# Sums of W_out made behind the memory in the first stage, in place of the second stage

## The chip, the cores and the metric

One core of one Trainium2 chip runs the whole kernel. The metric is the device time of one launch in microseconds (us). Three runs of the kernel before took 629.17, 630.27 and 633.15 us; the median is 630.27. The engines are named PE (TensorE), DVE (VectorE), ACT (ScalarE), POOL (GpSimd) and SP (SyncE, which here only issues transfers).

## The reference

One layer over 2048 tokens of width 1024, all in float32:

```
hn    = rms_norm(x) * norm_g
u | mq | gate = hn @ w_in                 # 768 | 256 | 1024 columns
tok   = pooled windows (2, 4, 8, 16) of u, minus u, times w_group, times scale
mem_o = softmax(mq @ mem_k.T / 8) @ mem_v # 4 heads, 256 memory rows
y     = x + (concat(tok, mem_o) * silu(gate)) @ w_out
out   = rms_norm(y) * final_g
```

## The kernel before, in words

Float32 products are made of three products of reduced parts: each operand is split into a high part (a cast, `_split`, mostly on ACT at L38) and a low part (a difference on DVE, L46), and PE does high x high, high x low and low x high (L51, L52, L53). So each tile of weights has to pass through ACT and DVE before PE can use it.

The tokens are four blocks of 512. Stage 1 projects blocks 0 and 1 tile by tile (`TILES`, `tile_in`): queries q, gates g and pooled columns z, each tile with 48 products of 128x512 for the two blocks. Stage 2 projects blocks 2 and 3 (`project_in`, `group`), two tiles at a time with seven products in place of eight, and then come the two output projections, the second again with seven products (`project_out_by_products`). Sums of W_out that four of those seven need are made by `stage_weights` and kept in DRAM as `t_d`; the matching sums of the input columns of blocks 2 and 3 are made by `stage_forms` during stage 1, after `row_stats` has made the norms of those blocks from squares on ACT (L221).

After each half tile a counter (`Steps`) is advanced, and side work hangs on its values through `hooks`: the norms of blocks 0 and 1, the fold of w_group into the projection (`w_z`), the memory's keys and values (`memory`, at 17), the norms of the second pair (`stats`), its forms (`stage`), and the attention steps. In this program the order of the source is not the order on an engine: a scheduler places all instructions by a simulated timeline. On the chip each engine then works through its own list strictly in order, and so do the DMA queues of SP, ACT and POOL. [...]

`load` makes the scheduler issue its transfers in the order of the calls. `slot(n)` names one of fourteen large buffers x0 to x13, `zz` one of four smaller ones. `gate` tiles end in a Silu on ACT (`take_gate`, L496 to L499), z tiles in window sums on POOL (L523) and DVE (L532, L538). Attention is scores (L581, L582), maximum (L584), exponentials (L588), division (L591, L593), transposes (L604), split (L606) and the product with the values (L616).

In the order of the tiles, g3 follows the memory, then come z5, g2, z4.

Of the kernel before, what the change touches and what calls it, by code (L numbers as in the profile page):

```python
# [8 lines left out]
F32 = mybir.dt.float32  # L9
# [6 lines left out]
P = 128  # L16
# [3 lines left out]
KH = KT // 2  # L20
BT = 512
# [20 lines left out]
def _split(nc, hi, lo, src, hi_eng, lo_eng="dve"):  # L42

    _cast(nc, hi_eng, hi, src)
    e = nc.gpsimd if lo_eng == "pool" else nc.vector
    return e.tensor_tensor(out=lo, in0=src, in1=hi.bitcast(F32), op=ALU.subtract)  # L46


def _mm3(nc, ps, ahi, alo, bhi, blo, start, stop, **kw):

    nc.tensor.matmul(ps, lhsT=ahi, rhs=bhi, start=start, stop=False, **kw)  # L51
    nc.tensor.matmul(ps, lhsT=ahi, rhs=blo, start=False, stop=False, **kw)  # L52
    nc.tensor.matmul(ps, lhsT=alo, rhs=bhi, start=False, stop=stop, **kw)  # L53
# [3 lines left out]
def trunk(ctx, tc, x, xT, mem, memT, norm_g, mem_norm_g, w_mem, w_out, w_in, w_uT, w_g, p_scale, final_g,  # L57
# [6 lines left out]
    sp = nc.sync  # L64
# [19 lines left out]
    def slot(n, shape=(P, KH, BT), dt=F32R):  # L84
        return sl.tile(list(shape), dt, name=f"x{n}")

    def zz(shape, dt=F32):

        n = 1
        for v in shape[1:]:  # L90
            n *= v
        t = zw.tile([P, HALO + D], dt, name="zz")[:, :n]
        if len(shape) == 3:
            t = t.rearrange("p (a b) -> p a b", a=shape[1])
        return t
# [22 lines left out]
    def load(**kw):  # L118

        if not last:  # L120
            last.append(sp.dma_start(**kw))
        else:
            with tc.issue_after(last[-1].ins):
                last.append(sp.dma_start(**kw))
        return last[-1]
# [71 lines left out]
    def rstd_of(ssq, n):  # L197
        v = small.tile([P, QT], F32, name="var")
        nc.vector.tensor_scalar(v[:, :n], ssq, 1.0 / D, EPS, ALU.mult, ALU.add)
        r = small.tile([P, QT], F32, name="rstd")  # L200
        nc.gpsimd.tensor_tensor(out=r[:, :n], in0=v[:, :n], in1=half[:, :n], op=ALU.pow)
        return r

    def bcast_cols(r, n, dst, rb=None):

        ps = (ps_t if n == QT else ps_mm).tile([P, BT], F32, name="pt" if n == QT else "mm")
        rb = (sgp.tile([P, BT], F32, name="sg") if rb is None else rb)[:, :n * P].rearrange("p (t f) -> p t f", t=n)
        nc.vector.tensor_copy(rb, r[:, :n].unsqueeze(2).broadcast_to([P, n, P]))
        for t in range(n):
            nc.tensor.matmul(ps[:, t * P:(t + 1) * P], lhsT=rb[:, t, :], rhs=ident, start=True, stop=True)  # L210
        nc.vector.tensor_copy(dst, ps[:, :n * P])
# [29 lines left out]
    def combine(b11, b12, b21, b22, t1, t2, t4):  # L241

        g = nc.vector
        sub(g, t1, b12, b11)
        sub(g, t2, b22, t1)
        sub(g, b12, b22, b12)
        sub(g, t4, b21, t2)
# [34 lines left out]
    def x_slots(ps):  # L282
        return {p: tuple(slot(n) for n in PLACE[p]) for p in ps}
# [71 lines left out]
    def memory_norm(loaded):  # L355
        ssm = small.tile([P, 2], F32, name="ssm", bufs=1)
        for t in range(2):
            nc.scalar.activation(out=loaded[1][t], in_=loaded[1][t], func=AF.Square, accum_out=ssm[:, t:t + 1])
        loaded.append(rstd_of(ssm, 2))

    def memory(loaded):
        mh, ml = ([zz((P, 4, NMEM), F32R) for _ in range(2)] for _ in range(2))
        wrs, _, rm = loaded
        for c in range(2):
            mt = mts[c]
            for kk in range(4):
                k = 4 * c + kk
                g = gm[:, k:k + 1]
                nc.scalar.mul(mh[c][:, kk, :], mt[:, kk, :], g)
                nc.vector.scalar_tensor_tensor(out=ml[c][:, kk, :], in0=mt[:, kk, :], scalar=g,  # L370
                                               in1=mh[c][:, kk, :].bitcast(F32), op0=ALU.mult, op1=ALU.subtract)
        pk = [pl.tile([P, NMEM], F32, name=n) for pl, n in ((ps_s, "sc"), (ps_t, "pt")) for _ in range(2)]
        for c in range(4):
            wr = wrs[c]
            for kk in range(2):
                k = 2 * c + kk
                hi, lo = chunk(wr[:, kk, :], "pool")
                xh, xl = mh[k // 4][:, k % 4, :], ml[k // 4][:, k % 4, :]
                for p in range(2):
                    w = slice(p * P, (p + 1) * P)  # L380
                    _mm3(nc, pk[p], hi[:, w], lo[:, w], xh, xl, k == 0, k == KT - 1)
                for t in range(2):
                    w = slice(t * P, (t + 1) * P)
                    _mm3(nc, pk[2 + t], xh[:, w], xl[:, w], hi[:, NMEM:], lo[:, NMEM:], k == 0, k == KT - 1)
        rmb = sgp.tile([P, BT], F32, name="sg")[:, :NMEM]
        bcast_cols(rm, 2, rmb)
        nc.vector.tensor_scalar_mul(rmb, rmb, 0.125)
        for p in range(2):
            kf = att.tile([P, NMEM], F32, name="pr")
            nc.vector.tensor_tensor(out=kf, in0=pk[p], in1=rmb, op=ALU.mult)  # L390
            for h in range(2):
                r, o = slice(64 * h, 64 * h + 64), slice(64 - 64 * h, 128 - 64 * h)
                _split(nc, khi[r, p, h, :], klo[r, p, h, :], kf[r], "act")
                nc.gpsimd.dma_start(out=khi[o, p, h, :].bitcast(F32), in_=khi[r, p, h, :].bitcast(F32))
                nc.gpsimd.dma_start(out=klo[o, p, h, :].bitcast(F32), in_=klo[r, p, h, :].bitcast(F32))
        for t in range(2):
            vf = att.tile([P, NMEM], F32, name="pr")
            nc.vector.tensor_scalar_mul(vf, pk[2 + t], rm[:, t:t + 1])
            src = vf.rearrange("p (a h d) -> p a h d", a=2, h=2)
            for h in range(2):  # L400
                hi, lo = slice(64 * h, 64 * h + 64), slice(64 - 64 * h, 128 - 64 * h)
                _split(nc, vhl[:, t, :, h, hi], vhl[:, t, :, h, lo], src[:, :, h, :], "act")

    def chunk(src, hi_eng, shape=(P, BT), lo_eng="dve"):

        hi = ch.tile(list(shape), F32R, name="wh")
        lo = ch.tile(list(shape), F32R, name="wl")
        _split(nc, hi, lo, src, hi_eng, lo_eng)
        return hi, lo
# [277 lines left out]
    def y_later(p):  # L687
        y_slots(p)
        for k in range(0, KH, 2):
            rt = raw_tile((P, 2, BT))  # L690
            sp.dma_start(out=rt, in_=ys_d[k:k + 2, :, LATER.index(p), :].rearrange("k p t -> p k t"))
            for kk in range(2):
                _split(nc, Y[p][0][:, k + kk, :], Y[p][1][:, k + kk, :], rt[:, kk, :], "act")

    def stage_weights(k):

        r = []
        for kk in (k, k + KH):
            r.append(zz((P, 2, BT)))
            for dh in range(2):  # L700
                sp.dma_start(out=r[-1][:, dh, :], in_=w_out[kk // 2, dh, :, kk % 2, :])
        t = zz((P, 2, BT))
        t4 = sgp.tile([P, BT], F32, name="sg")
        b11, b12, b21, b22 = r[0][:, 0, :], r[0][:, 1, :], r[1][:, 0, :], r[1][:, 1, :]
        combine(b11, b12, b21, b22, t[:, 0, :], t[:, 1, :], t4)
        for i, v in enumerate((t[:, 0, :], t[:, 1, :], b12, t4)):
            nc.gpsimd.dma_start(out=t_d[i, k // 2, :, k % 2, :], in_=v)
# [154 lines left out]
    loaded = []  # L862
# [27 lines left out]
    def stats(a):  # L890
        if not a:
            load(out=ci, in_=cinv)
            state["rows"] = dram.tile([2, QT, P], F32, name="rows")
        row_stats(1, a, state["rows"])

    def stage(k):
        if not X1:
            X1.update(x_slots((1, 6, 2)))
        stage_forms(1, k, state["rows"], X1)
# [6 lines left out]
    def norm(a):  # L906
        first_norm(a)
        for f in unscaled[a]:
            f()

    hooks = {7: [lambda: norm(0)], 10: [lambda: norm(1)], 12: [fold, lambda: ahead.append(load_tile(w_in[6], load)), lambda: loaded.extend(load_memory())],
             14: [lambda: load_memory_rest(loaded)],
             15: [lambda: memory_norm(loaded)], 17: [lambda: memory(loaded)], 19: [lambda: stats(0)], 21: [lambda: stats(1)]}
    for k in range(KH):
        hooks[25 + 9 * k] = [lambda k=k: stage(k)]
    steps = Steps(0, 21, 2.4, hooks)
    xs = {0: first_block(0)}
    for kind, j, blocks in TILES:
# [30 lines left out]
            branch(s, e, *bhl[s], lambda: (zz if by == "zz" else raw_tile)((P, 2, BT)))  # L949

    hooks = {NP - 4: [lambda: bring(0, 0, (0, 1, 2, 3), "zz")], NP - 2: [lambda: bring(0, 1, (4, 5, 6, 7), "zz")]}
    for k, n in enumerate((12, 26, 30, 34)):
        hooks[n] = [lambda k=k: stage_weights(k)]
    project_in(1, X1, Steps(1, 10, 2, hooks))

    AT_CHUNK = {(0, 2): 0, (0, 3): 1, (1, 0): 2, (1, 1): 3}
# [51 lines left out]
```

## Time and profile before

| | |
|---|---|
| median of three runs | 630.27 us |
| profiled execution | 632.58 us |
| its span | 630.3 us |
| mean granted TensorE clock | 0.973 |
| PE busy | 592.0 us, 94% of the span |
| DVE busy | 452.8 us, 72% |
| ACT busy | 336.0 us, 53% |
| POOL busy | 160.3 us, 25% |

The span is the time from the first to the last instruction; some 2 us of the device time lie around it. An engine's busy time counts its instructions alone. A wait in square brackets behind a row of a timeline is the time that the engine stood idle before that instruction, and the instruction or transfer that released it. [...]

### The profile page before, as it was taken

The numbers are of one execution on the slowest core, as the hardware profiler recorded it, in microseconds if no ns is written. First come the engines' busy times: TensorE is split into PE (matmuls) and PEld (weight loads), VectorE is DVE, ScalarE is ACT, GpSimd is POOL, SyncE is SP. The second block draws the span as 40 slices with busy tenths as digits, with TensorE's granted clock in tenths as the row PEclk, the third lists the DMA queues.
The fourth block names the chain that finished last, engine by engine and source line by source line (L and its number), as shares of the span: only waits on it lengthen the run. The fifth ranks groups of instructions, "written<-read, shape, count | busy, mean of one in ns | idle before, by whom it ended". The sixth has DMA issues, their size and how long they took to land. (4 is left out here: it accounts for less than half of the span.)

```text
span 630.3 us, 8543 instructions
## 1 busy us (share of the span) xinstructions
PE 592.0 (94%) x2798; PEld 490.9 (78%) x2798; DVE 452.8 (72%) x754; ACT 336.0 (53%) x696; POOL 160.3 (25%) x181
## 2 busy tenths in 40 slices
PE   7989779989989999999998899989899999999993
PEld 4879669868768888888886788868688888887882
DVE  6470246599786768897779888798785842969776
ACT  6825545446464664664963789634553511516442
POOL 0021114263442304101048212354100000304065
PEclk9999969999989999999999899989899999999998
DMA  8949995366465943668441986345999474799606
GB/s 314 391 166 338 393 356 170 117 198 227 161 236 160 319 146 112 234 219 294 165 112 48 294 296 216 125 145 198 353 359 351 135 244 144 236 358 344 221 19 248
DMA packets 63311, 144.34 MB, mean 229 GB/s; under 512 B 7714, under 2 KB 16674, under 8 KB 63268
## 3 DMA queue, kind: packets, MB, share of 16 engines
q1 hardware_dynamic: 53620, 122.30, 57.4%
q10 hardware_dynamic: 6832, 12.60, 5.4%
q0 software_dynamic: 2816, 8.92, 3.7%
q8 instruction: 22, 0.36, 0.2%
q14 instruction: 21, 0.17, 0.1%
HBM read 98.17 MB, written 45.09 MB: 227 GB/s over the span
## 5 line engine op out<-in xcount | busy, mean ns | idle before, releaser
L51 PE MATMUL mm<-x,wh 128*128 128x512 f32 x480 | 192.1, 402 | 11.1 <-ACT wh L38 8.2
L52 PE MATMUL mm<-x,wh 128*128 128x512 f32 x480 | 190.8, 398 | 0.6 <-DVE x L230 0.6
L53 PE MATMUL mm<-x,wl 128*128 128x512 f32 x480 | 189.7, 399 | 0.3 <-DVE wl L46 0.3
L46 DVE TENSOR_TENSOR wl<-raw,wh 128x512 fp32r<-128x512 f32 x116 | 86.6, 753 | 68.2 <-ACT wh L38 67.9
L38 ACT CAST wh<-raw 128x512 fp32r<-128x512 f32 x116 | 70.5, 617 | 89.7 <-PE pt L53 28.3
L51 PEld LDWEIGHTS mm<-x,wh 128*128 128x128 f32 x480 | 92.5, 193 | 31.2 <-ACT wh L38 8.6
L523 POOL TENSOR_TENSOR zz<-zz 128x527 f32<-128x527 f32 (+6 forms) x64 | 82.1, 1293 | 102.4 <-DVE zz L550 42.5
L52 PEld LDWEIGHTS mm<-x,wh 128*128 128x128 f32 x480 | 92.3, 192 | 19.8 <-DVE x L230 1.7
L53 PEld LDWEIGHTS mm<-x,wl 128*128 128x128 f32 x480 | 92.2, 192 | 19.4 <-DVE wl L46 1.1
L53 PE MATMUL mm<-wh,x 128*128 128x512 f32 x128 | 49.8, 389 | 0.0
L52 PE MATMUL mm<-wl,x 128*128 128x512 f32 x128 | 49.8, 389 | 0.0
L51 PE MATMUL mm<-wh,x 128*128 128x512 f32 x128 | 46.8, 390 | 2.0 <-ACT wh L38 2.0
L588 ACT ACTIVATE pr<-sc,nm 128x256 f32<-128x256 f32 x64 | 29.9, 472 | 29.9 <-DVE nm L584 26.0
L38 ACT CAST x<-raw 128x512 fp32r<-128x512 f32 x40 | 23.8, 617 | 37.6 <-DMA raw<-ys_d 12.4
L753 POOL TENSOR_TENSOR rstdo<-sso,half 128x1 f32<-128x1 f32 x16 | 12.7, 796 | 111.6 <-DVE sso L745 111.6
L593 ACT ACTIVATE pr<-pr,rc 128x256 f32<-128x256 f32 x64 | 29.1, 504 | 21.7 <-DVE rc L591 21.5
L46 DVE TENSOR_TENSOR x<-raw,x 128x512 fp32r<-128x512 f32 x40 | 32.8, 834 | 8.0 <-ACT x L38 8.0
L51 PEld LDWEIGHTS mm<-wh,x 128*128 128x128 f32 x128 | 24.0, 188 | 7.3 <-ACT wh L38 2.4
L52 PEld LDWEIGHTS mm<-wl,x 128*128 128x128 f32 x128 | 24.0, 188 | 5.0
L53 PEld LDWEIGHTS mm<-wh,x 128*128 128x128 f32 x128 | 24.0, 188 | 5.0
L604 PE MATMUL pt<-ident,pr 128*128 128x128 f32 x128 | 21.7, 288 | 6.2 <-ACT pr L593 6.1
L604 PEld LDWEIGHTS pt<-ident,pr 128*128 128x128 f32 x128 | 15.9, 146 | 11.3 <-ACT pr L593 8.7
(188 smaller groups left out, 1068.1 us busy)
## 6 DMA issues: line engine op xcount, KB each, us to landing
raw<-in_w_in SPq DMA_DIRECT2D x19, 512.0 KB, 6.1
x<-in_x SPq DMA_DIRECT2D x16, 512.0 KB, 7.6
g_d<-sg ACTq DMA_DIRECT2D x32, 256.0 KB, 3.4
raw<-in_w_out SPq DMA_DIRECT2D x14, 512.0 KB, 4.4
raw<-w_z SPq DMA_DIRECT2D x12, 512.0 KB, 4.6
sg<-g_d SPq DMA_DIRECT2D x24, 256.0 KB, 3.2
br_d<-zz SPq DMA_DIRECT2D x12, 512.0 KB, 4.3
x<-in_xT SPq DMA_DIRECT2D x8, 512.0 KB, 7.6
```

Source lines behind the costliest of these rows:

```text
L38: return nc.scalar.copy(hi, src)
L46: return e.tensor_tensor(out=lo, in0=src, in1=hi.bitcast(F32), op=ALU.subtract)
L51: nc.tensor.matmul(ps, lhsT=ahi, rhs=bhi, start=start, stop=False, **kw)
L52: nc.tensor.matmul(ps, lhsT=ahi, rhs=blo, start=False, stop=False, **kw)
L53: nc.tensor.matmul(ps, lhsT=alo, rhs=bhi, start=False, stop=stop, **kw)
L523: nc.gpsimd.tensor_tensor(out=cur[rows, c0:c1], in0=prev[rows, c0:c1], in1=prev[rows, c0 - step:c1 - step], op=ALU.add)
L588: nc.scalar.activation(out=pr[:, h, :], in_=ps[:, h, :], func=AF.Exp, bias=nm[:, h:h + 1], accum_out=su[:, h:h + 1])
L593: nc.scalar.mul(pr[:, h, :], pr[:, h, :], rc[:, h:h + 1])
L604: nc.tensor.transpose(ps[:, 2 * h + kt, :], pr[:, h, kt * P:(kt + 1) * P], ident)
L753: nc.gpsimd.tensor_tensor(out=ro, in0=self.sso[:, 1, t:t + 1], in1=half[:, :1], op=ALU.pow)
```

## The change

`stage_weights(k)` for k = 0 to 3 is called at step 18 of stage 1, four times in a row, right after the memory; before, it was called at steps 12, 26, 30 and 34 of stage 2. It takes its input from slots x8, x9, x11 and x13 and puts the sums into x10 and x12, which are empty at that time, and not into `zz` buffers; its loads go through `load`. The norms of the second pair move from steps 19 and 21 to 22 and 24, and its forms from steps 25, 34, 43 and 52 to 29, 37, 45 and 53. Nothing is added or left out: the same loads, differences and stores are made.

```diff
+    sums = []
+
     def stage_weights(k):
 
-        r = []
-        for kk in (k, k + KH):
-            r.append(zz((P, 2, BT)))
+        b = slot((8, 9, 11, 13)[k], (P, 2, 2, BT), F32)
+        r = [b[:, i] for i in range(2)]
+        for kk, v in zip((k, k + KH), r):
             for dh in range(2):
-                sp.dma_start(out=r[-1][:, dh, :], in_=w_out[kk // 2, dh, :, kk % 2, :])
-        t = zz((P, 2, BT))
+                load(out=v[:, dh, :], in_=w_out[kk // 2, dh, :, kk % 2, :])
+        if k % 2 == 0:
+            sums.append(slot((10, 12)[k // 2], (P, 2, 2, BT), F32))
+        t = sums[-1][:, k % 2]
         t4 = sgp.tile([P, BT], F32, name="sg")
...
-             15: [lambda: memory_norm(loaded)], 17: [lambda: memory(loaded)], 19: [lambda: stats(0)], 21: [lambda: stats(1)]}
+             15: [lambda: memory_norm(loaded)], 17: [lambda: memory(loaded)], 18: [lambda: [stage_weights(k) for k in range(KH)]],
+             22: [lambda: stats(0)], 24: [lambda: stats(1)]}
     for k in range(KH):
-        hooks[25 + 9 * k] = [lambda k=k: stage(k)]
+        hooks[29 + 8 * k] = [lambda k=k: stage(k)]
...
-    for k, n in enumerate((12, 26, 30, 34)):
-        hooks[n] = [lambda k=k: stage_weights(k)]
```

The scheduler's lists move around tile z5 and the tile after it, g2. On ACT before, from the cast of the second half of g3 (`wh_958`) to g3's second gate; `wh_1025` and `wh_1098` are z5's weights, `wh_1182` g2's, `x12` and `x13` rows of block 3, `sg_1013` a gate:

```order
L38 CAST wh_958<-raw_734 128x512
L221 ACTIVATE x12_1061,ss_1068<-x12_1061 128x1024
L38 CAST wh_1025<-raw_1021 128x512
L221 ACTIVATE x13_1064,ss_1068<-x13_1064 128x1024
L38 CAST khi_165<-pr_914 64x256 x2
L38 CAST khi_165<-pr_924 64x256 x2
L38 CAST wh_1098<-raw_1021 128x512
L221 ACTIVATE x13_1064,ss_1068<-x13_1064 128x1024
L38 CAST wh_1182<-raw_1178 128x512
L38 CAST vhl_167<-pr_934 128x2x64 x2
L38 CAST vhl_167<-pr_940 128x2x64 x2
L498 ACTIVATE sg_1013<-sg_1013 128x512
```

On ACT now, from the same gate (`sg_1044`) to the first cast of g2's weights (`wh_1240`):

```order
L498 ACTIVATE sg_1044<-sg_1044 128x512
L221 ACTIVATE x11_1109,ss_1113<-x11_1109 128x1024
L221 ACTIVATE x11_1109,ss_1113<-x11_1109 128x1024
L588 ACT_TABLE_LOAD
L588 ACTIVATE pr_1154,su_1155<-sc_1147,nm_1152 128x256 x2
L498 ACT_TABLE_LOAD
L593 ACTIVATE pr_1154<-pr_1154,rc_1158 128x256 x2
L221 ACTIVATE x12_1183,ss_1190<-x12_1183 128x1024
L221 ACTIVATE x13_1186,ss_1190<-x13_1186 128x1024
L38 CAST pth_1162<-pt_1164 128x4x128
L588 ACT_TABLE_LOAD
L38 CAST wh_1240<-raw_1236 128x512
```

The rows left out between these are more of the same kinds: in all there stand between the gate and that cast six squares, three pairs of exponentials, three pairs of scalings, three table loads, a second Silu and one cast of probabilities. Before, the cast of g2's weights stood ahead of the gate, and all squares of the second pair ahead of both gates.

On DVE now, from the last differences of `stage_weights` (L102) to the product that the gate's Silu waits for (`sg_1044`, L496); `wl_1057` and `wl_1132` are the low parts of z5's weights, `zz_1208` takes z5's result for the first block (`mm_1054`):

```order
L102 TENSOR_TENSOR x13_1002<-x13_1002 128x512
L398 TENSOR_SCALAR pr_934<-pt_776,rstd_712 128x256
L398 TENSOR_SCALAR pr_940<-pt_777,rstd_712 128x256
L46 TENSOR_TENSOR wl_1057<-raw_1052,wh_1056 128x512
L46 TENSOR_TENSOR wl_1132<-raw_1052,wh_1131 128x512
L46 TENSOR_TENSOR vhl_167<-pr_934,vhl_167 128x2x64 x2
L46 TENSOR_TENSOR vhl_167<-pr_940,vhl_167 128x2x64 x2
L102 TENSOR_TENSOR sg_1007<-x13_1002,x12_992 128x512
L550 TENSOR_TENSOR zz_1208<-mm_1054,u_322 128x512
L496 TENSOR_TENSOR sg_1044<-mm_736,u_322 128x512
```

Before, the same product (`sg_1013<-mm_736`) stood ahead of the copy of z5's first block (`zz_1150<-mm_1023`), with ten rows between them; now it stands behind it.

On SP before, the transfers from z5's weights (`raw_1021`) to the first column load of the second pair; `raw_1178` are g2's weights:

```order
L124 DMA raw_1021<-w_z_164 128x1024
L124 DMA x12_1061<-in_x 128x1024 x2
L124 DMA x13_1064<-in_x 128x1024 x2
L124 DMA raw_1178<-in_w_in 128x1024
L265 DMA raw_1245<-in_xT 128x2x512
```

On SP now, from the first loads of W_out to g2's weights (`raw_1236`):

```order
L124 DMA x9_973<-in_w_out 128x512 x4
L124 DMA x11_987<-in_w_out 128x512 x4
L124 DMA x13_1002<-in_w_out 128x512 x4
L124 DMA raw_1052<-w_z_164 128x1024
L124 DMA ci_162<-in_cinv 128x96
L124 DMA x10_1106<-in_x 128x1024 x2
L124 DMA x11_1109<-in_x 128x1024 x2
L124 DMA x12_1183<-in_x 128x1024 x2
L124 DMA x13_1186<-in_x 128x1024 x2
L124 DMA raw_1236<-in_w_in 128x1024
```

The rows of blocks 2 and 3 now go into slots in which W_out and its sums have been, so their loads wait until these have been stored.

## Rows read from the trace of the kernel before

**Rows 1.** Page, part 1: engine, busy us, share of the span, instructions.

```profile
PE 592.0 (94%) x2798; PEld 490.9 (78%) x2798; DVE 452.8 (72%) x754; ACT 336.0 (53%) x696; POOL 160.3 (25%) x181
```

**Rows 2.** What PE waited for over the whole span: us in total, times, longest.

```profile
PE pt L604 <- ACT pr L593: 6.1, 3, 2.9
PE sc L616 <- DVE ptl L46: 5.0, 2, 2.7
```

**Rows 3.** Windows of 10 us: busy us by engine, then granted clock, DMA share, GB/s.

```profile
80.00:90.00 10.00, 6.49 (x25) 5.55 (x26) 4.08 (x8) 5.42 (x10) 0.00 (x0) 0.58 0.99 358
140.00:150.00 10.00, 10.00 (x43) 8.34 (x43) 9.71 (x18) 5.16 (x12) 0.56 (x1) 0.85 0.60 188
```

**Rows 4.** Timeline of PE at the memory: start, us, operation, [idle before <- releaser].

```profile
83.51 0.80 PE L51 MATMUL mm<-x,wh 128*128 128x512 f32 x1 [8.20 <-ACT wh L38]
...
87.94 0.58 PE L52 MATMUL mm<-x,wh 128*128 128x512 f32 x1
88.36 0.39 PE L53 MATMUL mm<-x,wl 128*128 128x512 f32 x1
88.59 0.39 PE L51 MATMUL mm<-x,wh 128*128 128x512 f32 x1
```

**Rows 5.** Timeline of ACT at the memory.

```profile
82.42 0.33 ACTq L499 DMA_DIRECT2D g_d<-sg  x1
82.84 0.62 ACT L38 CAST wh<-raw 128x512 fp32r<-128x512 f32 x1 [2.05 <-DMA x<-in_x]
```

**Rows 6.** Timeline of PE: first products of tile z5 and of tile g2.

```profile
109.49 0.39 PE L51 MATMUL mm<-x,wh 128*128 128x512 f32 x1
...
122.73 0.39 PE L51 MATMUL mm<-x,wh 128*128 128x512 f32 x1
```

**Rows 7.** Timeline of ACT from g2's first weight cast to the next table load.

```profile
109.46 0.62 ACT L38 CAST wh<-raw 128x512 fp32r<-128x512 f32 x1 [1.61 <-PE mm L52]
...
128.52 0.91 ACT L593 ACTIVATE pr<-pr,rc 128x256 f32<-128x256 f32 x2 [4.34 <-DVE rc L591]
129.34 1.13 ACT L38 CAST wh<-raw 128x512 fp32r<-128x512 f32 x2
130.37 0.47 ACT L588 ACTIVATE pr<-sc,nm 128x256 f32<-128x256 f32 x1
...
131.28 0.61 ACT L38 CAST x<-raw 128x512 fp32r<-128x512 f32 x1
...
149.23 1.28 ACT L498 ACT_TABLE_LOAD   x1
150.53 0.63 ACT L498 ACTIVATE sg<-sg 128x512 f32<-128x512 f32 x1
```

**Rows 8.** Groups of ACT by form: squares of rows; busy us, mean ns, idle before.

```profile
L221 ACT ACTIVATE x<-x 128x1024 f32<-128x1024 f32 x16 | 16.9, 1056 | 4.2 <-DMA x<-in_x 3.8
```

**Rows 9.** Timeline of SP: the load of g2's weights.

```profile
88.32 0.51 SPq L124 DMA_DIRECT2D raw<-in_w_in  x1
```

**Rows 10.** Timelines of DVE and PE around the wait at 139.06, and PE at 183.71.

```profile
134.09 4.31 DVE L46 TENSOR_TENSOR x<-raw,x 128x512 fp32r<-128x512 f32 x1
...
139.06 0.38 PE L616 MATMUL sc<-ptl,vhl 128*128 128x256 f32 x1 [2.69 <-DVE ptl L46]
...
183.71 1.09 PE L604 MATMUL pt<-ident,pr 128*128 128x128 f32 x4 [2.92 <-ACT pr L593]
```

**Rows 11.** Timelines of DVE and PE in stage 2, at a load of W_out.

```profile
356.82 0.69 DVE L102 TENSOR_TENSOR zz<-zz 128x512 f32<-128x512 f32 x1 [2.46 <-DMA zz<-in_w_out]
...
358.17 0.50 PE L53 MATMUL mm<-x,wl 128*128 128x512 f32 x1 [0.33 <-DVE wl L46]
...
362.06 0.38 PE L581 MATMUL sc<-khi,mq 128*128 128x256 f32 x1 [1.22 <-ACT pr L588]
```

**Rows 12.** Transfers of the whole span: KB each, median us from issue to landing.

```profile
x<-in_x SPq DMA_DIRECT2D x16, 512.0 KB, 7.6
...
t_d<-zz POOLq DMA_DIRECT2D x12, 256.0 KB, 4.5
```

## The prediction

> **What bounds the kernel now.** I read the page's busy shares first: TensorE (PE) is busy for 592.0 of the 630.3 us [rows 1], so at most some 38 us can be won, and any time in which PE stands is lost unless a later stall shrinks by it. Next the list of what PE waited for: attention's probabilities from ScalarE (ACT), three times, 6.1 us, and the low parts of the transposed probabilities from VectorE (DVE), twice, 5.0 us [rows 2]. The largest wait by itself is 8.20 us at the memory, where PE waits for a weight cast by ACT [rows 4]. Then the windows of 10 us, for the granted clock [rows 3], and last the ACT and DVE timelines around these places. The reader is to see that PE is fed by two in-order engines: a cast that stands late in ACT's order stops PE, however idle ACT is on average.
>
> A stall costs more than itself. After the 8.20 us one, matmuls stand 0.42 us apart (87.94, 88.36) and 0.23 us apart only from 88.36 on [rows 4]; the window shows a granted clock of 0.58 [rows 3]. From 83.51 to 88.36 PE did in 4.85 us what takes 4.85 x 0.23/0.42 = 2.6 us: 2.3 us lost. After the 2.69 us stall at 139.06 [rows 10] the next 10 us had 0.85 of the clock [rows 3]: 1.5 us lost.
>
> **The change, part by part.**
>
> *At the memory.* The cast that ends the 8.20 us wait stands on ACT behind a gate's store: store at 82.42, cast at 82.84 [rows 5]. [...]
>
> *The sums in stage 1.* Sixteen differences at 0.69 us at most (the one at 356.82 [rows 11]) are some 11 us of DVE work beside the memory products. PE is covered while those products last; behind them the low part of tile z5's weights stands on DVE after the last differences. Counting what stands ahead of it I put z5's start 1.35 us late, with 0 and 3 us as bounds. The t_d stores, on the GpSimd queue, land after 4.5 us [rows 12] and nobody on PE reads them before the last stage.
>
> *Tile g2, the term that decides.* Before, the cast of g2's first weights runs at 109.46 [rows 7], ahead of the gate's Silu and of attention, and g2's weights were asked for at 88.32 [rows 9]; g2 follows z5 on PE at 122.73 without a wait [rows 6]. Now that cast stands behind the whole first round of attention and behind the squares of the second pair, and the Silu at the head of that chain waits for a DVE product that DVE does only behind its copy of z5's first block. So the chain cannot start before PE is nearly done with z5, and PE has nothing between z5 and g2 but a few scores and transposes.
>
> z5 started at 109.49 [rows 6]. Now: 1.4 earlier, 1.35 later, and 0.8 earlier because a round of broadcast matmuls is no longer ahead of it: 108.6. Its 48 matmuls at 0.2275 and two score matmuls (0.2) end at 119.8. Its first block is done 12 matmuls (2.7) earlier; a copy and the Silu's product on DVE take 0.69 each at most, as a difference does [rows 11]: 1.4. ACT's chain starts at 118.5. In it stand, in ACT's order: 2 Silu (0.63 each [rows 7]), 6 squares of rows at 1.05 [rows 8], 3 table loads at 1.28 [rows 7], 3 pairs of exponentials (130.37 to 131.28, 0.91 a pair [rows 7]), 3 pairs of scalings (128.52 to 129.34, 0.82 [rows 7]) and one cast of probabilities, 0.6 as a weight cast [rows 7]. That is 1.26 + 6.30 + 3.84 + 2.73 + 2.46 + 0.6 = 17.2, then the cast itself, 0.6: g2's weights are ready at 118.5 + 17.2 + 0.6 = 136.3. Attention's part of it is not on top: PE's transposes wait inside the same chain. The squares of the last rows need loads that stand behind the sums' stores; I put their issue at about 114, and with 7.6 us [rows 12] they land ahead of ACT's arrival at about 127.
>
> g2 starts at 136.3 in place of 122.73, a lag of **13.6 us**. PE's own small work after z5 I put at 2.4 us, so it stands for about 14 us, and the clock costs about as much as after the 8.20 us stall: **2.3 us**. Bounds for the pair: 9 us (the first squares done before the chain is released and the scalings not in the way) and 20 us.
>
> [...]
>
> *What comes back in stage 1.* The 2.69 us stall at 139.06 is a DVE stall: a split took 4.31 us at 134.09 [rows 10] while GpSimd ran z5's window sums, and the transposed low part waited behind it. Those window sums depend on z5, which ends no later than before, while what PE needs of DVE is 13 us later: the clash falls into the gap. I take off 2.7 and its 1.5 of clock: **-4.2 us** (bounds 0 and -8.6: the wait of 2.92 at 183.71 [rows 10] going too, with 1.5 of clock). What is late next is ACT with those probabilities; its order there is nearly as before, so I leave that wait in.
>
> *Stage 2.* The differences, their loads and stores leave. On PE's path I find one: DVE waits 2.46 us for a load of W_out at 356.82, and PE then waits 0.33 and 1.22 us [rows 11]: **-1.55 us** (bounds 0 and -9: the second wait for low parts, 2.3, and one of those for probabilities, 2.5 [rows 2], going too with 1.5 of clock each).
>
> **Sum.** 13.6 + 2.3 - 4.2 - 1.55 = +10.1 us. The profiled execution took 632.58, 2.3 above the median of 630.27; it would become 642.7, and against the median **640**.
>
> **Rivals.** A: as summed, 636.6 to 646, with 640 the likeliest. For it: three in-order engines give the same order at g2, whatever the durations. Against: one event carries it.
>
> B: the lag is given back. While PE stands, ACT and DVE run ahead, and the three waits for probabilities, 6.1 us [rows 2], go as well, with 1.5 us of clock behind each of the two long ones: 640 - 9.1 = 631, no change to be told. For it: these are exactly ACT's work. Against: ACT's order puts that work after g2's casts.
>
> C, on the other side: the chain on ACT is released early and g2's cast is hidden. This is so if the copy of z5's first block runs some 11 us before z5's end and not 2.7, which needs PE to take z5 block by block, or if z5 starts 13 us later than I count while the Silu is free. Then only the gains stand: 1.4, 4.2 and 1.55, and, with DVE relieved in stage 2, up to 7.8 more: 615 to 623, say 621. The new order of PE alternates the blocks of z5, which speaks against it.
>
> D: the differences, now beside GpSimd's weight casts at the memory, are slowed as the split at 134.09 was (4.31, where a difference takes 0.69 [rows 10, 11]). One such on the way to the memory's products gives 3.6 us and the clock: 645 to 648. For it: both engines work on the same stretch now. [...]
>
> **Chances.** A 0.50, B 0.26, C 0.11, D 0.13. A change under 1% (6.3 us) can't be told from none here. Slower by over 1% (above 636.6): nearly all of A, and D: 0.61. Within: B and a little of A: 0.28. Faster (below 624): C: 0.11. The range goes from 629, which takes in B, to 648, which takes in D, and leaves out C and some tails.
>
> **What would show it.** In the profile after: a wait of PE of 11 to 16 us between about 120 and 137, ended by ACT's weight cast at the start of g2, with a granted clock of about 0.6 in the 10 us around its end; the 8.20 us wait at 6 to 8; no 2.7 us wait for the transposed low part in stage 1; no DVE wait for W_out in stage 2, where PE's waits of 0.33 and 1.22 are gone. Wrong it is if g2's first matmul follows z5 within 4 us (C), or if the gap is there and the three waits for probabilities are not (B).

## The result, and the profile after

The changed kernel took 643.23 us (median of four runs, 641.57 to 644.52), the kernel before 631.5 beside it: a ratio of 1.015 with a 95% interval of 1.012 to 1.018, 11.7 us slower. A repeat in a later set of runs gave 644.69 against 633.63, 1.018 (1.013 to 1.023). The span of the profiled execution is 642.7 us where that of before is 630.3, 12.4 more.

In the extracts below, `...` marks rows that are left out. What PE waited for, after (us in total, times, longest); the rows answer to [rows 2]:

```profile
PE mm L51 <- ACT wh L38: 15.8, 3, 7.0
PE sc L581 <- ACT pr L588: 6.4, 3, 2.9
PE sc L616 <- DVE ptl L46: 2.8, 2, 2.4
PE pt L210 <- DVE s L208: 2.1, 1, 2.1
PE pt L604 <- ACT pr L593: 1.6, 3, 0.8
```

PE waits longer for weight casts (15.8 us, before 10.2) and for exponentials (6.4, before 1.2) and, new, for a broadcast norm; its waits for divided probabilities shrank from 6.1 to 1.6. PE's timeline places the longer ones:

```profile
83.11 0.79 PE L51 MATMUL mm<-x,wh 128*128 128x512 f32 x1 [6.87 <-ACT wh L38]
...
110.15 0.63 PE L51 MATMUL mm<-x,wh 128*128 128x512 f32 x1 [1.91 <-ACT wh L38]
...
126.80 0.39 PE L581 MATMUL sc<-khi,mq 128*128 128x256 f32 x1 [2.87 <-ACT pr L588]
...
129.60 2.07 PE L210 MATMUL pt<-ident,s 128*128 128x128 f32 x8 [2.06 <-DVE s L208]
...
139.50 0.79 PE L51 MATMUL mm<-x,wh 128*128 128x512 f32 x1 [6.97 <-ACT wh L38]
...
228.38 0.39 PE L581 MATMUL sc<-khi,mq 128*128 128x256 f32 x1 [2.67 <-ACT pr L588]
...
363.00 0.58 PE L616 MATMUL sc<-ptl,vhl 128*128 128x256 f32 x1 [2.38 <-DVE ptl L46]
...
441.21 0.61 PE L51 MATMUL mm<-x,wh 128*128 128x512 f32 x1 [2.84 <-DVE u L105]
```

z5 starts at 110.15, g2 at 139.50, where [rows 6] have 109.49 and 122.73. Between 123 and 139.5 PE stands three times, 11.9 us in all. ACT is busy for 16.41 of the 16.50 us of that stretch, and its rows come in the order of its list, as forecast; over the whole span it makes 32 table loads where the kernel before makes 28:

```profile
121.69 0.63 ACT L498 ACTIVATE sg<-sg 128x512 f32<-128x512 f32 x1 [4.88 <-DVE sg L496]
...
124.43 1.28 ACT L588 ACT_TABLE_LOAD   x1
...
128.46 1.28 ACT L498 ACT_TABLE_LOAD   x1
...
134.79 1.28 ACT L588 ACT_TABLE_LOAD   x1
...
138.84 2.17 ACT L38 CAST wh<-raw 128x512 fp32r<-128x512 f32 x4
```

The windows around it show the clock (busy us by engine, granted clock, DMA share, GB/s):

```profile
130.00:140.00 10.00, 3.03 (x13) 2.62 (x13) 4.71 (x9) 9.97 (x22) 4.07 (x5) 0.50 0.59 213
140.00:150.00 10.00, 10.00 (x42) 8.14 (x41) 4.36 (x8) 1.60 (x3) 0.00 (x0) 0.77 0.31 101
```

ACT works 9.97 of 10 us while PE works 3.03, at a granted clock of 0.50 (it is 1.00 in the kernel before from 88.36 on, where products stand 0.23 us apart [rows 4]); in the next window PE works all 10 us and ACT 1.60. These two rows show the wait at g2; how it came about is for the experiments.

How far each kernel is behind the kernel before is read by matching the n-th product of a tile (line 51) of the two traces, a figure worked out from their start times. From g3 on, a tile of stage 1 has 16 of these products; stage 2 begins at n = 256, at 264.5 us in the kernel before:

| n | start before, us | lag after, us | what lies there |
|---|---|---|---|
| 64 | 83.5 | -0.4 | the memory |
| 80 | 109.5 | +0.7 | z5 starts |
| 96 | 122.7 | +16.8 | g2 starts |
| 112 | 134.6 | +21.5 | g2 is done, z4 starts |
| 120 | 146.5 | +15.1 | behind the wait at 139.06 of before |
| 192 | 212.3 | +12.0 | behind the wait at 183.71 of before |
| 208 | 225.1 | +17.5 | behind the wait at 228.38 of after |
| 368 | 357.1 | +16.0 | the middle of stage 2's tiles |
| 384 | 373.0 | +13.1 | behind the last sums of before |
| 479 | 459.7 | +12.5 | end of the tiles |

### The profile page after: what moved, and what is told of

The parts are those of the page before. It is cut to its first block, busy times and chain, and to the rows that moved or that the text cites. A ratio compares the mean times of both kernels' runs of the same rounds, so it can differ in the third digit from the quotient of the medians.

```text
span 642.7 us, 8533 instructions
## 1 busy us (share of the span) xinstructions
PE 594.6 (93%) x2798; PEld 493.8 (77%) x2798; DVE 453.5 (71%) x754; ACT 341.6 (53%) x700; POOL 163.1 (25%) x181
## 3 DMA queue, kind: packets, MB, share of 16 engines
q0 software_dynamic: 2816, 8.92, 3.5%
## 4 chain that ended last, share of the span: by engine, by line
PE 47%; DVE 17%; DMA 15%; issue 9%; ACT 7%; POOL 3%; SPq 1%; ACTq 0%; POOLq 0%; DVEq 0%
PE mm L51 11%; PE mm L52 11%; PE mm L53 11%; DMA raw<-w_z 3%; DVE wl L46 3%; DMA raw<-t_d 3%; DMA x<-in_w_out 2%; DVE zz L538 2%; PE sc L52 2%; PE sc L53 2%; PE pt L52 1%; PE pt L53 1%; DVE x L46 1%; ACT wh L38 1%; PE sc L51 1%
## 5 line engine op out<-in xcount | busy, mean ns | idle before, releaser
L51 PE MATMUL mm<-x,wh 128*128 128x512 f32 x480 | 192.6, 404 | 22.7 <-ACT wh L38 15.8
L46 DVE TENSOR_TENSOR wl<-raw,wh 128x512 fp32r<-128x512 f32 x116 | 88.8, 772 | 72.9 <-ACT wh L38 66.4
L51 PEld LDWEIGHTS mm<-x,wh 128*128 128x128 f32 x480 | 92.7, 193 | 43.4 <-ACT wh L38 17.5
L523 POOL TENSOR_TENSOR zz<-zz 128x527 f32<-128x527 f32 (+6 forms) x64 | 85.1, 1341 | 144.8 <-ACT zz L548 75.7
L46 DVE TENSOR_TENSOR x<-raw,x 128x512 fp32r<-128x512 f32 x40 | 30.5, 777 | 7.6 <-ACT x L38 7.6
L593 ACT ACTIVATE pr<-pr,rc 128x256 f32<-128x256 f32 x64 | 29.0, 502 | 12.5 <-DVE rc L591 12.4
L38 ACT CAST pth<-pt 128x512 fp32r<-128x512 f32 x32 | 18.7, 584 | 18.9 <-PE pt L604 18.4
L38 ACT CAST x<-zz 128x512 fp32r<-128x512 f32 x32 | 18.4, 619 | 13.3 <-DMA zz<-br_d 5.0
```

Of the source, the lines that this page charges most:

```text
L38: return nc.scalar.copy(hi, src)
L523: nc.gpsimd.tensor_tensor(out=cur[rows, c0:c1], in0=prev[rows, c0:c1], in1=prev[rows, c0 - step:c1 - step], op=ALU.add)
L593: nc.scalar.mul(pr[:, h, :], pr[:, h, :], rc[:, h:h + 1])
```

## The experiments

Two theories stood at the start. T: what costs is ACT's order at g2, which is so because the sums push norms and their squares behind them. W: it is the sums' own work, 4 MB of loads and 16 differences beside the memory, wherever anything else stands. A third, N, put it on the later steps of norms and forms. In the course of it a fourth, L, was set beside T: the rows of the second pair go into the slots of the sums, so their loads wait until the sums are stored, and everything that hangs on the rows is late. Each time stands beside that of the kernel before in the same set of runs (631.03 to 634.33). Of the edits only the lines that matter are shown.

**g2's weights asked for early.**

```
-  18: [lambda: [stage_weights(k) for k in range(KH)]],
+  18: [lambda: early_load("g", 2), lambda: [stage_weights(k) for k in range(KH)]],
```

`early_load` calls `load_tile` and keeps the tile for `tile_of`.

> The changed kernel with one load moved: g2's weights are asked for just before the sums' first load, and nothing else in the source differs. The scheduler then puts g2's two weight casts on ACT ahead of the gate's Silu and of the squares. Theory T (the cast of g2's weights stands late in ACT's order): PE's three waits before g2, 2.87 + 2.06 + 6.97 = 11.9 us, shrink to below 4, with the 2 us of clock behind them, so 629 to 634. Rival W (it is the sums' work itself in stage 1, 16 differences on DVE and 4 MB of loads in the same stretch, that takes the time, whatever ACT's order): the time stays at 640 to 645.

Measured: 637.78 against 634.33, 1.005 (1.002 to 1.008). The waits at g2 are gone (n = 96 is at -0.4 against before). The edit moves the load of g2's weights and, with it, the place of their cast, so it doesn't tell which of the two made that wait. A third of the loss stays, and it shows some 30 us on. PE, ACT and DVE of this run:

```profile
156.12 0.58 PE L581 MATMUL sc<-khi,mq 128*128 128x256 f32 x1 [6.61 <-ACT pr L588]
```

```profile
155.05 0.47 ACT L588 ACTIVATE pr<-sc,nm 128x256 f32<-128x256 f32 x1 [1.89 <-DVE nm L584]
```

```profile
148.18 2.15 DVE L267 SCALAR_TENSOR_TENSOR raw<-raw,gx,s 128x512 f32<-128x512 f32 x2 [2.54 <-DMA s<-rows]
...
154.34 0.68 DVE L584 TENSOR_REDUCE nm<-sc 128x2 f32<-128x512 f32 x1
```

Read upwards: DVE waited for the norms (`s<-rows`), did the forms that need them, and only then the maximum that ACT's exponentials and PE's scores wait for. The norms are late in this kernel too. T as first put, with the cast alone, is too small.

**The norms ahead of the sums.**

```
-  18: [lambda: [stage_weights(k) for k in range(KH)]],
-  22: [lambda: stats(0)], 24: [lambda: stats(1)]}
+  19: [lambda: stats(0)], 21: [lambda: stats(1)],
+  24: [lambda: [stage_weights(k) for k in range(KH)]]}
```

> The changed kernel with the norms of the second pair back at steps 19 and 21 and the sums behind them, at step 24 of stage 1; forms as in the changed kernel. On ACT the casts of g2's weights then stand behind both gates' Silu but ahead of attention and behind no square. Theory T: no wait of over 3 us before g2, 626 to 633. Rival W (the sums' work in stage 1 as such): 638 to 645, since all of that work is still in stage 1, only 6 steps later.

Measured: 620.95 against 634.33, 0.978 (0.973 to 0.983): the fastest of all, with the same work in stage 1. So W falls as the cause of the loss. It went below what T gave. SP's timeline of the changed kernel, then of this one:

```profile
90.89 8.66 SPq L124 DMA_DIRECT2D x<-in_w_out  x12
99.87 0.43 SPq L124 DMA_DIRECT2D raw<-w_z  x1
...
106.91 15.42 SPq L124 DMA_DIRECT2D x<-in_x  x8
122.38 0.44 SPq L124 DMA_DIRECT2D raw<-in_w_in  x1
```

```profile
73.75 2.89 SPq L124 DMA_DIRECT2D x<-in_x  x4
...
86.44 1.76 SPq L124 DMA_DIRECT2D x<-in_x  x4
88.25 1.90 SPq L124 DMA_DIRECT2D x<-in_w_out  x4
...
95.40 11.69 SPq L124 DMA_DIRECT2D x<-in_w_out  x12
107.13 0.43 SPq L124 DMA_DIRECT2D raw<-in_w_in  x1
```

The rows of the second pair are asked for from 73.75 on, and not from 106.91 to 122.33 with SP standing between them. Their squares then run on ACT from 83.40 to 104.5, where it has only a few casts beside them. What SP waited for in the changed kernel names the stores of the sums:

```profile
SPq L124 <- DMA t_d<-x: 17.4, 4, 8.1
```

Such a wait stands in the trace of each version that has the sums ahead of the norms (17.4 to 19.2 us, without the differences 9.0), and in none of the others.

The kernel before asks for its rows as early as this version (from 73.69 on), so that takes the loss away but doesn't explain a time below the kernel before. That comes from waits of the kernel before that are gone here: it gains 4.6 us where the wait of 2.69 us [rows 10] stood (n = 112 to 120), and 8.7 us in stage 2 (-2.8 at n = 256, -11.6 at n = 479), where waits of 2.36, 2.46 and 1.99 us and the two of [rows 11] are gone. The prediction's C had put the change without the lag at 621.

**The sums alone, and the moves alone.** The first has the diff's `stage_weights` at 18 with the old steps of norms and forms; the second has the new steps with the sums left in stage 2.

> One part of the change alone: the sums at step 18 of stage 1, with the norms and forms at the steps of the kernel before (19, 21 and 25, 34, 43, 52). On ACT the cast of g2's weights still stands behind four squares, two pairs of exponentials and two of scalings, with one table load in place of three: 10 us of chain in place of 17. Theory T: a wait at g2 remains, 4 to 8 us with its clock, 634 to 640. Rival N (the later steps of norms and forms are what costs): 628 to 632.

> The other part of the change alone: norms at steps 22 and 24 and forms at 29, 37, 45, 53, with the sums made in stage 2 as in the kernel before. On ACT the cast of g2's weights stands ahead of both gates, as before. Theory T: no wait at g2, 627 to 634, the time of the kernel before. Rival N (the later steps are what costs): 638 to 645.

Measured: sums alone 647.85, 1.020 (1.014 to 1.025), moves alone 630.33, 0.993 (0.990 to 0.996), both against 634.33. N falls: the later steps cost nothing, they even win 0.7%, which is won at the memory, where PE's wait is 5.12 us and no longer 8.20 (n = 64 is at -2.5, n = 479 at -2.1). The sums alone lose more than T gave, and at z5 already, of which PE and SP show, and, as the third extract, SP's row for the same load in the kernel before:

```profile
122.06 0.80 PE L51 MATMUL mm<-x,wh 128*128 128x512 f32 x1 [8.52 <-ACT wh L38]
```

```profile
106.28 5.19 SPq L124 DMA_DIRECT2D x<-in_x  x4
111.52 0.47 SPq L124 DMA_DIRECT2D raw<-w_z  x1
```

```profile
84.12 0.34 SPq L124 DMA_DIRECT2D raw<-w_z  x1
```

Here z5's weights stand on SP behind the row loads that wait for the sums' stores, and are asked for at 111.52 and not at 84.12. So with the norms called at 19, ahead of z5's tile in the chain of loads, the same late rows hold up z5 in place of g2.

**Shorter squares; no differences.** Two single costs taken out of the changed kernel. The first leaves 7/8 of each sum of squares out, the second stores the quarters of W_out unsummed; both compute other values and serve for their time alone.

```
-  nc.scalar.activation(out=rows[t], in_=rows[t], func=AF.Square, accum_out=ss[:, t:t + 1])
+  c = rows[t] if full else rows[t][:, :P]        # full is False for the second pair
+  nc.scalar.activation(out=c, in_=c, func=AF.Square, accum_out=ss[:, t:t + 1])
```

```
-  combine(b11, b12, b21, b22, t[:, 0, :], t[:, 1, :], t4)
-  for i, v in enumerate((t[:, 0, :], t[:, 1, :], b12, t4)):
+  for i, v in enumerate((b11, b21, b12, b22)):
```

> The changed kernel with the squares of the second pair over 128 of their 1024 columns (7/8 of each sum of squares is left out); loads, sums and order are those of the changed kernel, on ACT nearly row for row. Theory T (the squares, pushed behind the sums, stand in ACT's chain ahead of g2): six squares in that chain take 0.3 in place of 1.05 us, so PE's three waits before g2 fall from 11.9 to 7 to 8 us, and the time by 4 to 6.5 us against the changed kernel, which is 12 above the kernel before: 5.5 to 8 above it. Rival L (what counts is when the rows and weights land, behind the sums' stores; ACT would have waited anyway): less than 2 us off, 10 to 12 above the kernel before.

> The changed kernel without the 16 differences of stage_weights (the loaded quarters of W_out are stored as they are, so the last stage works on unsummed weights); all loads and stores stay, and the norms still come behind them. Rival W (DVE's work on the sums beside the memory is what costs): the lag at g2 goes, time at or below that of the kernel before. Rival L and theory T (the rows' loads wait for the stores out of the slots, so the squares come late, into attention's chain): a lag at g2 of 8 us or more remains, and the time stays 6 to 12 us above the kernel before.

Measured: short squares 640.88 against 634.05, 1.010 (1.006 to 1.014), 6.8 above the kernel before; no differences 645.96, 1.019 (1.016 to 1.022), 11.9 above. The short squares came as T said (5.5 to 8 above the kernel before) and not as L (10 to 12); the kernel without differences came as both said, and against W. ACT's chain with short squares:

```profile
121.17 0.63 ACT L499 ACTIVATE sg<-sg 128x512 f32<-128x512 f32 x1 [3.74 <-DVE sg L497]
...
134.31 2.16 ACT L38 CAST wh<-raw 128x512 fp32r<-128x512 f32 x4
```

It lasts 13.1 us in place of 17.15, and PE's three waits are 8.4 in place of 11.9, a little above the 7 to 8 expected. So at g2 PE waited for the length of ACT's chain, and the squares in it are part of that. But the load is late too: in the changed kernel g2's weights are asked for at 122.38 and, by the trace's landing times, land at 131.39. With 0.66 us from cast to product, g2 could not have started before some 132.0, an estimate from these rows, and z5 ends at 123.1. Of the 16.4 us from there to 139.50 some 9 would have stood with ACT free, and the chain put 7.4 on top. No run has one of the two without the other.

Without the differences DVE is busy 10.4 us less (443.1 for 453.5), and g2 starts 20.3 us behind the kernel before (n = 96). That run is 2.5 us behind at the memory already (n = 64), where the changed kernel is 0.4 ahead; from there to g2 the two lose 17.8 and 17.2. So nothing is won without the differences.

**g3's weights ahead of the memory's loads,** on top of the norms ahead of the sums (`early_load("g", 3)` at step 12, before `load_memory`).

> The version with the norms ahead of the sums, and with g3's weights asked for ahead of the memory's loads and not behind them. PE's longest wait that is left there, 8.37 us at the memory for the cast of g3's weights, should go, as the cast then stands on ACT ahead of the memory's own work. If nothing else stands behind it, 5 to 10 us less: 607 to 613 where the kernel before takes 631 to 634. If the memory's operands, which the same saturated queue brings, are late by as much, PE waits for them instead and less than 3 us are won: 617 to 621.

Measured: 632.21, 0.995 (0.992 to 0.999). The 8.4 us wait at the memory is gone, n = 80 is 11.2 us ahead of before; 24 of the counted products on, n = 104 is 6.1 behind. PE reached g2 before its weights and norms did:

```profile
112.87 1.16 PE L210 MATMUL pt<-ident,s 128*128 128x128 f32 x8 [2.68 <-DVE s L208]
...
118.73 0.58 PE L581 MATMUL sc<-khi,mq 128*128 128x256 f32 x1 [3.75 <-ACT pr L588]
...
126.73 0.80 PE L53 MATMUL mm<-x,wl 128*128 128x512 f32 x1 [4.51 <-DVE wl L46]
```

Neither expectation held: the memory's operands were in time, but what was late stood a tile further on, and the version lost 11 us against the one without the early load. ACT stood here too, for 7.56 us up to 105.40, as in the second run of the next group.

**g2's weights early too,** with the norms ahead of the sums: once without and once with g3's early load (`early_load("g", 2)` at step 24, before the sums).

> The version with the norms ahead of the sums, with g2's weights asked for ahead of the sums' loads. There PE has no wait at g2 to lose, so nothing is won: 619 to 623 where the kernel before takes 631 to 635. If the load order alone decided, as against the norms' place, 3 us or more would be won or lost.

> Both early loads: g3's weights ahead of the memory's loads and g2's ahead of the sums' loads, with the norms ahead of the sums. With g3's alone PE was 11 us ahead at 109 and lost 18 us at g2 in waits for the broadcast norms (2.7), the exponentials (3.8) and g2's low parts (4.5). If these come of g2's weights being asked for at 109.7, behind the sums' loads, they go, and the 11 us are kept: 608 to 614. [...]

Measured: 625.70, 0.990 (0.987 to 0.994), and 628.89, 0.995 (0.992 to 0.998), against 631.03. The first misses its range and falls on its other branch (3 us or more won or lost), the second lies 15 us above its range: the 11 us were not kept. The first is 4.7 us behind the run without the early load (7 to 8 if each is taken against the kernel before of its own set), and all of that is in stage 2: at n = 272 the two are 3.6 and 2.9 ahead of before, at n = 479 6.2 and 11.6. Its trace has waits of 2.38 at 344 and 2.84 at 423 that the other has not; why the order of stage 2 comes out otherwise was not tested. In the second, ACT stood idle ahead of a gate's store:

```profile
106.20 0.33 ACTq L499 DMA_DIRECT2D g_d<-sg  x1
106.57 1.06 ACT L221 ACTIVATE x<-x 128x1024 f32<-128x1024 f32 x1 [8.92 <-DMA mq<-q_d]
```

ACT does nothing for 8.92 us, up to 106.57, and the profile names a load of queries as what ended it; neither the store, issued at 106.20, nor the square behind it reads these queries. Why the two wait for that load was not shown, and a version without it there was not tried.

**The sums behind the norms, forms at the old steps; and two repeats.** The first is the norms-first version with `hooks[25 + 9 * k]`.

> The sums in stage 1 behind the norms (step 24), with the norms and forms at the steps of the kernel before; against the run with the sums alone at step 18, which took 647.85, only their step differs. Rows' loads and squares are then ahead of the sums. Theory L (the place of the sums against the norms decides): 618 to 628 where the kernel before takes 631 to 634, some 20 us below the run with the sums at step 18. Rival W (the sums' work in stage 1 as such): 640 or more.

> The best version so far once more, beside the changed kernel on the same chip: 619 to 623. It had no wait of 2.4 us for low parts near 347 and none of 2.8 us for a sum on DVE near 435, which the changed kernel and the variant with g2's early load both show; if these come and go with the order of DVE and not from run to run, they are absent again.

> The changed kernel once more, on the chip of the other two: 641 to 645, 11 to 13 us above the kernel before.

Measured, against 633.63: 635.86, 1.003 (1.001 to 1.006); 621.02, 0.981 (0.977 to 0.984); 644.69, 1.018 (1.013 to 1.023). The repeats agree with the first runs, and the two waits of stage 2 are absent again from the version with the norms first, so they go with the order. The first missed its range: with the sums at 24 and the forms at 25, right behind them, z4's weights are late, and PE waits 1.66, 1.32 and 2.27 us between 139 and 145 and 3.32 at 178. The six cases side by side, as medians and ratios:

| sums at | forms at 25, 34, 43, 52 | forms at 29, 37, 45, 53 |
|---|---|---|
| 18, ahead of the norms | 647.85 (1.020) | 643.23, 644.69 (1.015, 1.018) |
| 24, behind the norms | 635.86 (1.003) | 620.95, 621.02 (0.978, 0.981) |
| stage 2 | the kernel before (1) | 630.33 (0.993) |

In the upper row the norms stand at 19 and 21 on the left and at 22 and 24 on the right, below at 19 and 21 (22 and 24 for the sums in stage 2, on the right). Of these cases the sums in stage 1 pay only in the one where rows and norms go ahead of them and the forms keep clear behind. Other steps were not run, and neither was a version that puts the sums into buffers that the rows don't use. In such a program each edit also moves the scheduler's lists elsewhere, stage 2 among them, so a difference of a few us between two cells need not come from the sums.

## Why the prediction was right

The direction, the place and the main term came out: 11.7 us slower where 10.1 stood. That the sum lies so near is in part luck, as the steps show:

- *At the memory.* The wait forecast at 8.2 - 1.4 = 6.8 is 6.87, and the releaser of the cast is now a load of W_out, where it was a load of rows [rows 5]:

```profile
82.44 0.62 ACT L38 CAST wh<-raw 128x512 fp32r<-128x512 f32 x1 [2.20 <-DMA x<-in_w_out]
```

  But the size is luck: no run shows the term of 1.4. That load landed at 82.00 and the cast came at 82.44, 0.4 us earlier than before (82.84); the rest is that PE came to the wait 0.9 us later in this execution (n = 63). The cast does not read W_out; why it waits for that load was not shown.
- *z5.* Forecast at 108.6, 1.35 us late for a low part on DVE. It started at 110.15, after a wait of 1.91 us for the cast of its weights, which had landed only then: their load stands behind twelve loads of W_out on SP (99.87 above).

```profile
109.48 1.14 ACT L38 CAST wh<-raw 128x512 fp32r<-128x512 f32 x2 [2.84 <-DMA raw<-w_z]
```

  The size was within the bounds (0 to 3), the reason was wrong, and a loss of clock came on top: the granted clock is 1.00 up to 110.15 and 0.53 from there to 113.6, and products stand 0.43 us apart there, against 0.23. That costs 1.6 us more, and z5 ended 3.3 us behind the 119.8 of the sum.
- *ACT's chain.* Forecast 17.2 us from Silu to g2's cast; measured 121.69 to 138.84, 17.15. Each of the three table loads is 1.28 us long, and the next instruction starts 0.01 to 0.02 us behind its end (125.72, 129.76 and 136.09). The loads of the last rows were issued at 120.51 to 122.33 and not at 114, and the last landed at 130.16, still ahead of the last square (137.00).
- *g2.* Forecast 136.3, measured 139.50, all of it from the late gate, whose product on DVE no run moves by itself. The lag is 16.8 where 13.6 stood. PE stood 11.9 us and not 14, since its scores and broadcasts lay between the pieces of the wait. The sum has no term for the load of g2's weights, which landed at 131.39: the chain was the longer of two legs, and the prediction had the right one.
- *The clock behind it.* 2.3 forecast. Products stand 0.43 us apart from 139.50 to 144.4, 4.9 us at a granted clock of 0.50, 2.3 lost. The lag grows by 4.7 up to n = 112, so some 2.4 of it is no clock but rounds of broadcasts, transposes and attention products that fall into g2 now. (In the prediction, 4.85 x 0.23/0.42 is 2.66, so the loss behind the 8.20 us wait is 2.2 and not 2.3.)
- *What comes back in stage 1.* Forecast 4.2; the lag falls by 6.4 behind the place of the 2.69 us wait, which is gone, so that surplus comes back too. The wait of 2.92 [rows 10] shrank as well (3.1 us from n = 120 to 192), which the sum had left in. Against it stands one that I did not foresee, 2.67 us at 228.38 and 5.5 of lag: a gate's Silu stands in ACT's order between two exponentials of one head pair, with a table load on either side. ACT's rows there:

```profile
222.64 1.28 ACT L588 ACT_TABLE_LOAD   x1
...
224.52 1.28 ACT L498 ACT_TABLE_LOAD   x1
...
226.46 1.28 ACT L588 ACT_TABLE_LOAD   x1
```

  Three loads in 5.1 us, with PE waiting for the second exponential.
- *Stage 2.* Forecast 1.55. The waits of 0.33 and 1.22 [rows 11] are gone and the lag falls by 2.9 between n = 368 and 384; the wait of 2.36 for a low part is there as before (2.38 at 363.00). Of the others two went (2.46 for probabilities at 420, 1.99 for a weight cast at 449) and one came (2.84 at 441.21). From n = 208 to the end 5 us came back, 0.4 of it still in stage 1; that is inside the bound of 9.

The sum was +10.1, the spans differ by 12.4. Against the forecast the terms came out at +3.2 (g2's lag), +2.4 (what follows it up to the end of g2), -5.3 (what stage 1 gave back, 9.5 in place of 4.2), +5.5 (the wait at 228.38, missed) and -3.5 (behind it, stage 2 in the main, 5.0 in place of 1.55): +2.3, in which misses of 9 and 11 us cancel. What the experiments show as the cause is the place of the sums ahead of the norms. The prediction has one side of it as its main term (the squares lengthen ACT's chain ahead of g2's cast, which the short squares bear out) and the other only as a side remark (the rows' loads wait for the sums' stores, and the weights queued behind them are late). How much each is worth at g2 is worked out above and not tested. B's mechanism, stalls that go because ACT and DVE catch up, was real for the waits at 139 and 184 and gave back 9.5 of the lag's peak of 21.5 in stage 1. By the prediction's own sign against itself, the gap there and the three waits for probabilities gone, the trace lies between A and B: those waits fell from 6.1 to 1.6 us, but waits for exponentials grew from 1.2 to 6.4, and the total stayed with A. D's is excluded as the cause: without the differences nothing was won.

## What to carry to other kernels

Work moved into empty buffers is not free if the next user of those buffers is on the way to the bound engine: look who loads into them next, and put the earlier-needed one first. Taking the wait before a tile away, by an early load, only moved the wait to a later tile in two runs here (g2's weights early, g3's weights early); such a fix pays when all that the bound engine needs for the following tiles is on time. Where an engine takes its list in order, as ACT's rows from 121.69 to 138.84 show it here, walk the list from the instruction that releases a long chain to the one that the bound engine waits for, and add the measured durations: here that gave 17.2 for 17.15 us. Put the landing of the bound engine's own load beside it (131.39 here, against a cast at 138.84), since the later of the two decides.

## What was not expected of the hardware

In three traces ACT stood idle ahead of a gate's store and the instruction behind it, and the profile names as what ended the wait a transfer that SP had issued and that neither of the two reads: 8.92 and 7.56 us in two runs, 2.20 at the memory in the changed kernel. After a wait of only 1.91 us, at 110.15, PE's products stood 0.43 us apart for 3.4 us, at a granted clock of 0.53; behind the wait of 8.20 [rows 4] they stood 0.43 us apart up to 88.36, at 0.50. PE had worked 7.96 of the 8.2 us ahead of the wait of 1.91, at a granted clock of 1.00. The waits of 0.6 to 1.2 us between 160 and 220 in the fastest version are followed by no such rows: products stand 0.23 to 0.24 us apart behind them. And a change of order, with the same loads, differences and stores, moved this kernel between 621 and 648 us.
